# Both merge-gate products of a hybrid decoder layer in the seven-product scheme, with sums made on the fly

## The chip, the cores and the metric

The kernel runs on one core of one Trainium2 chip. The metric is the device time of one execution in microseconds (us). The kernel before takes 618.91 us, the median of three runs (618.71 to 619.36).

## The reference, cut to what matters

The layer takes 512 tokens of 1024 channels (float32). It normalises them to `h`, projects `h`, runs two branches (a gated linear recurrence giving `y_a` and a latent attention giving `y_b`, both 512 x 1024), and merges the branches by two sigmoid gates:

```python
h      = rms_norm(x, norm_g)
proj   = h @ w_in                       # its last 2 * 1024 columns are glog
gates  = sigmoid(glog + b_gate).reshape(B, S, 2, D_MODEL)
merged = gates[:, :, 0] * (y_a @ w_proj_a) + gates[:, :, 1] * (y_b @ w_proj_b)
x      = x + merged @ w_out
return rms_norm(x, final_norm_g)
```

The change is about the two products that make `glog`: 512 x 1024 times 1024 x 1024, once for each gate.

## The kernel before, in words

Every large product is made of three matmuls per block: each operand is split into a high part (rounded to the matmul's reduced float32 format) and a low part (the rest), and high x high, high x low and low x high are summed in PSUM. A split of a weight is one cast on ACT (`split` L155, `load_w` L113) and one subtraction on DVE (L156, L114). The normalised tokens lie split and transposed in `hT` (8 blocks of 128 channels by 512 tokens, high and low).

`proj_ch` (L122) is the ordinary product: for 256 output columns it loads two weight pieces of 512 KB, splits them, and issues 48 matmuls of 128 x 128 weights with 512 tokens streamed (lines 90 to 92). `gates` (L709) calls it four times for a gate and puts tanh on the result (ACT, L715). So one gate is 192 matmuls of 512 columns.

`ch_product` (L870) is one product of the seven-product (Strassen) scheme: the 1024 x 1024 weight is cut in four 512 x 512 blocks and the 512 tokens in two halves of 256; seven products of block sums replace eight. One product is 48 matmuls with 256 tokens streamed. In the kernel before two products use the scheme: `y_a @ w_proj_a` (L914 to 931) and, by tokens, `merged @ w_out` (L1078 to 1107). Their block sums are made by DMAs that add into SBUF (`add_by_dma`, L800, POOL's queue).

The order of the end of the kernel before:

- attention, head by head; for the last head (`h + 1 == H`, L760) PE's order is written by hand: gate 0's first 256 columns, with the transposes of the last head's softmax (`mla_transpose`, L696) in the middle, then `mla_out` (lines 90 to 92 with `pt` and `v`)
- the other three column groups of gate 0 (L849), during which `ya` is split and summed and the blocks of `w_proj_a` are loaded (L791) and summed by DMA
- `w_proj_a` by the seven products, PE by hand
- `merge` (L938): for each of four column groups, gate 1's `proj_ch`, then `w_proj_b`'s `proj_ch`; meanwhile the blocks of `w_out` are loaded into `ya`, `yb` and two further tiles and summed by DMA
- `w_out`'s seven products, the residual and the last norm.

Each engine runs its instructions in the order in which the scheduler queued them. Four buffers each hold high and low weight pieces (`whi`, `wlo`), three hold raw pieces (`wraw`), so two products' weights are held at a time. PSUM has three banks for products (`mm_ps`) and five for the rest (`ax_ps`). Tiles of a later stage (`Pool`, "left" and "right") lie on memory that earlier tiles leave; the first write waits for the last reader of what lay there.

Of the kernel before, what the change touches and what calls it, by code (L numbers as in the profile page):

```python
# [9 lines left out]
F32 = mybir.dt.float32  # L10
F32R = mybir.dt.float32r
# [7 lines left out]
P = 128  # L19
# [19 lines left out]
def hybrid_layer(ctx: ExitStack, tc: tile.TileContext, a):  # L39
# [698 lines left out]

    mw = Pool("mla", "right")
    ybp = Pool("ybp", "left")  # L740
    yb = ybp.tile([P, H, S], F32, "yb")
    qp, nope, pn = early
    late = None
    for h in range(H):
        pools = (ma_pool, mw)
        if h:
            pn = mla_scores(h, pools[h % 2], *nope, qp, h + 1 == H)
        if h + 1 < H:
            if h % 2:
                qp = mla_rope((h + 1) // 2)  # L750
        if h:
            z = mla_gate(h)
        if h:
            if h + 1 < H:
                nope = mla_nope(h + 1, pools[(h + 1) % 2])
            mla_out(*late)
            if h % 4 == 0:
                v = mla_values(h)
        hook = lambda: mla_transpose(pn)
        if h + 1 == H:  # L760
            with tc.manual_schedule(engines={mybir.EngineType.PE}):
# [63 lines left out]
    def a_tile(nm):  # L830
        return [yap.tile([P, 4, 256], F32R, f"{nm}{i}") for i in range(2)]
# [5 lines left out]
    def branch_blocks():  # L837

        return [yap.tile([P, 4, 512], F32, f"x{i}") for i in range(4)]

    x1, x2, x3, x4 = branch_blocks()
    p11, p12, p22, s1, s2 = [a_tile(n) for n in ("p11", "p12", "p22", "s1", "s2")]
    y11, y12, y21, y22 = blocks(ya)
    w_pa = a["w_proj_a"][0]
    with tc.issue_after(last_split[0].ins):
        for src, to in ((y11, p11), (y12, p12), (y22, p22)):
            a_parts(src, to)
    g = first_gates
    for c in range(1, 4):  # L849
        g = g + gates(0, c, to=ma)  # L850
        if c == 1:
            load_block(x3, w_pa, 0, 1)
            load_block(x1, w_pa, 0, 0)
            for q in kh:
                minus(y22[:, q], y22[:, q], y21[:, q])
                split(s1[0][:, q], s1[1][:, q], y22[:, q])
                minus(y21[:, q], y11[:, q], y21[:, q])
# [294 lines left out]
```

## Time and profile before

| | before |
|---|---|
| median of three runs | 618.91 us |
| profiled execution, its own time | 619.32 us |
| its span, first to last instruction | 617.6 us |
| PE (TensorE matmul) busy | 98% |
| DVE (VectorE) busy | 65% |
| ACT (ScalarE) busy | 42% |
| POOL (GpSimd) busy | 19% |
| mean granted TensorE clock | 0.997 |
| read from HBM, written | 60.25 MB, 2.10 MB |

Rows of the profile name a line of the kernel (L878), an engine, an operation, and out<-in by the program's tile names. PEld is PE's weight load, which overlaps the matmuls. SPq, ACTq and POOLq are the queues from which DMAs are issued. A matmul's own duration holds its way through the array; what a matmul costs in a stream is the distance from one to the next. Times "at 413.7" are microseconds from the start of the span. The profiled execution is 0.41 us above the median, and 1.7 us of its time lie outside its span.

### The profile page before, as it was taken

How to read it: one execution, taken by the hardware profiler on the slowest of the kernel's cores; microseconds unless marked ns; L12 is line 12 of the kernel's file. 1: busy time of each engine (PE TensorE's matmuls, PEld its weight loads, DVE VectorE, ACT ScalarE, POOL GpSimd, SP SyncE). 2: the span in 40 equal slices, each digit the busy share in tenths (PEclk: the TensorE clock that was granted, in tenths of full speed). 3: DMA queues.
4: the chain of work that ended last, by engine and by line, in shares of the span. 5: the costliest groups of instructions: out<-in, count | busy, mean ns of one | idle time of the engine just before them, and what ended most of it. 6: DMA issues, size and time to landing. Idle time of an engine off the chain costs nothing.

```text
span 617.6 us, 8947 instructions
## 1 busy us (share of the span) xinstructions
PE 607.3 (98%) x3400; PEld 518.2 (84%) x3400; DVE 400.5 (65%) x633; ACT 260.4 (42%) x483; POOL 117.9 (19%) x219
## 2 busy tenths in 40 slices
PE   8999999999999999999999999999999999999995
PEld 4998888888888888888888888888899888888884
DVE  7727855498874639967677757458267742447895
ACT  5645143323144232346545555354354532334352
POOL 3106201231230032321314132101110012000021
PEclk9999999999999999999999999999999999999998
DMA  8325243223205202432232243239952799600403
GB/s 275 117 67 171 68 140 100 68 69 103 69 12 160 80 24 59 116 86 74 72 99 74 55 117 88 70 84 325 239 148 51 270 359 276 193 1 0 171 0 136
DMA packets 62377, 72.35 MB, mean 117 GB/s; under 512 B 6104, under 2 KB 48510, under 8 KB 62336
## 3 DMA queue, kind: packets, MB, share of 16 engines
q1 hardware_dynamic: 58476, 61.37, 31.9%
q0 software_dynamic: 2160, 7.87, 6.4%
q10 hardware_dynamic: 1700, 2.56, 1.4%
q8 instruction: 26, 0.43, 0.3%
q14 instruction: 15, 0.12, 0.1%
HBM read 60.25 MB, written 2.10 MB: 101 GB/s over the span
## 4 chain that ended last, share of the span: by engine, by line
PE 96%; DVE 2%; ACT 1%; DMA 0%; issue 0%; POOL 0%; POOLq 0%; ACTq 0%; DVEq 0%
PE mm_ps L90 23%; PE mm_ps L91 23%; PE mm_ps L92 23%; PE ax_ps L878 6%; PE ax_ps L986 4%; PE ax_ps L675 2%; PE mm_ps L266 2%; PE ax_ps L696 1%; PE ax_ps L536 1%; PE ax_ps L92 1%; PE ax_ps L91 1%; PE ax_ps L90 1%; PE mm_ps L878 1%; PE mm_ps L986 1%; PE ax_ps L538 1%; PE ax_ps L498 1%
## 5 line engine op out<-in xcount | busy, mean ns | idle before, releaser
L114 DVE TENSOR_TENSOR w_lo<-w_raw,w_hi 128x1024 fp32r<-128x1024 f32 (+3 forms) x86 | 101.8, 1187 | 104.9 <-ACT w_hi L113 97.7
L113 ACT CAST w_hi<-w_raw 128x1024 fp32r<-128x1024 f32 (+3 forms) x86 | 85.0, 991 | 160.0 <-PE mm_ps L91 89.7
L90 PE MATMUL mm_ps<-hT,w_hi 128*128 128x512 f32 x384 | 151.2, 394 | 0.0
L91 PE MATMUL mm_ps<-hT,w_hi 128*128 128x512 f32 x384 | 150.0, 391 | 0.0
L92 PE MATMUL mm_ps<-hT,w_lo 128*128 128x512 f32 x384 | 149.6, 391 | 0.0
L92 PEld LDWEIGHTS mm_ps<-hT,w_lo 128*128 128x128 f32 x384 | 72.1, 188 | 14.8
L90 PEld LDWEIGHTS mm_ps<-hT,w_hi 128*128 128x128 f32 x384 | 72.2, 188 | 14.5 <-DVE qn L156 0.2
L91 PEld LDWEIGHTS mm_ps<-hT,w_hi 128*128 128x128 f32 x384 | 72.2, 188 | 14.2
L92 PE MATMUL mm_ps<-w_hi,hT 128*128 128x512 f32 (+1 forms) x96 | 36.6, 383 | 0.0
L91 PE MATMUL mm_ps<-w_lo,hT 128*128 128x512 f32 (+1 forms) x96 | 36.5, 382 | 0.0
L90 PE MATMUL mm_ps<-w_hi,hT 128*128 128x512 f32 (+1 forms) x96 | 36.4, 386 | 0.0
L683 POOL TENSOR_SCALAR p<-p,sm 128x128 f32<-128x128 f32 (+3 forms) x28 | 17.0, 608 | 71.1 <-DVE sm L680 60.6
L681 ACT ACTIVATE p<-ax_ps,sm 128x128 f32<-128x128 f32 (+3 forms) x32 | 16.9, 530 | 28.0 <-DVE sm L680 26.5
L455 DVE RECIPROCAL tf<-pr 128x512 f32<-128x512 f32 x8 | 26.8, 3351 | 0.2
L90 PE MATMUL mm_ps<-yb,w_hi 128*128 128x512 f32 x64 | 24.9, 389 | 0.0
L91 PE MATMUL mm_ps<-yb,w_hi 128*128 128x512 f32 x64 | 24.9, 389 | 0.0
L92 PE MATMUL mm_ps<-yb,w_lo 128*128 128x512 f32 x64 | 24.9, 389 | 0.0
L90 PE MATMUL mm_ps<-cT,w_hi 128*128 128x512 f32 x52 | 20.7, 398 | 0.0
L92 PEld LDWEIGHTS mm_ps<-w_hi,hT 128*128 128x128 f32 x96 | 18.0, 188 | 3.0
L90 PEld LDWEIGHTS mm_ps<-w_hi,hT 128*128 128x128 f32 x96 | 18.0, 188 | 3.0
L91 PEld LDWEIGHTS mm_ps<-w_lo,hT 128*128 128x128 f32 x96 | 18.0, 188 | 2.9
L92 PE MATMUL mm_ps<-cT,w_lo 128*128 128x512 f32 x52 | 20.3, 390 | 0.0
(284 smaller groups left out, 1147.1 us busy)
## 6 DMA issues: line engine op xcount, KB each, us to landing
w_raw<-w_in SPq DMA_DIRECT2D x58, 512.0 KB, 3.8
x<-w_proj_a SPq DMA_DIRECT2D x10, 512.0 KB, 6.5
x<-x POOLq DMA_DIRECT2D x8, 512.0 KB, 9.4
w_raw<-w_proj_b SPq DMA_DIRECT2D x8, 512.0 KB, 9.9
w_raw<-w_proj_a SPq DMA_DIRECT2D x4, 512.0 KB, 11.2
ya<-w_out SPq DMA_DIRECT2D x4, 512.0 KB, 7.7
t<-w_out SPq DMA_DIRECT2D x4, 512.0 KB
yb<-w_out SPq DMA_DIRECT2D x4, 512.0 KB, 10.9
```

The costliest lines, as they stand in the source:

```text
L90: nc.tensor.matmul(ps, lh[lsl], rh[rsl], start=start, stop=False)
L91: nc.tensor.matmul(ps, lh[lsl], rl[rsl], start=False, stop=False)
L92: nc.tensor.matmul(ps, ll[lsl], rh[rsl], start=False, stop=stop)
L113: nc.scalar.copy(hi[:, :o], raw[:, :o])
L114: (lo_eng or nc.vector).tensor_tensor(lo[:, :o], raw[:, :o], hi[:, :o].bitcast(F32), op=ALU.subtract)
L266: nc.tensor.matmul(ps, hT[l][:, 4 * kh + k, t * P : t * P + P], c_hl[kh][r][:, k * 256 : k * 256 + 256], start=kh == 0 and kind == 0 and k ...
L455: nc.vector.reciprocal(rp[:], pr[:])
L675: nc.tensor.matmul(sps[:, :n], qh[:, bl], kpe[x][:, :n], start=False, stop=x == 1)
L681: nc.scalar.activation(p[:, :n], sps[:, :n], AF.Exp, scale=SCALE, bias=sm[:, 1:2], accum_out=sm[:, 2:3])
L683: (nc.vector if final else nc.gpsimd).tensor_scalar(p[:, :n], p[:, :n], sm[:, 3:4], 0.5, op0=ALU.mult, op1=ALU.mult)
L878: nc.tensor.matmul(ps[:, o], w[k // 2][i][:, k % 2, cols], ap[j][:, k], start=not banks and c == 0 and n == 0, stop=n == 11, skip_group_ch ...
L986: nc.tensor.matmul(ps[:, o : o + n], ap[i][:, k, t * P : t * P + P], w[k // 2][j][:, k % 2, o : o + n], start=fresh and c == 0, stop=c == ...
```

## The change

`gates` goes; both gates are made with `strassen`, a function that holds the order of the seven products for gate 0, gate 1 and `w_proj_a` alike. `strassen` works on one set of four weight blocks `x4` (1 MB each, `x0` to `x3` for the blocks 00, 01, 10, 11). Their sums are made in place by POOL (`plus`: two adds of 128 x 1024 per block) and each block, once split, is loaded again with the block of the next matrix (`renew`): gate 0, then gate 1, then `w_proj_a`. The token sums of `h` (`s1` to `s4`) are made once, with `whole` (POOL: high + low) and DVE, and serve both gates.

For gate 0 the first two products (`w11` with `h11`, `w21` with `h12`) stand where gate 0's first column group stood, around the last head's transposes, and come from `load_w`. The third product, `t1` times `s1`, needs the sum `x0 + x1` and the token sum `s1 = h22 - h21`.

```diff
-    def gates(b, c, hook=None, to=None):
-
-        res = []
-        for i, ps in enumerate(proj_ch(w_in, COL_G + b * D + c * 256, hT, hook)):
...
+    def plus(out, x, y):
+        for q in kh:
+            nc.gpsimd.tensor_tensor(out[:, q], x[:, q], y[:, q], op=ALU.add)
+
+    def strassen(x, ops, out, first=None, between=(), mat=None, nxt=None):
...
+        y11, y12, y22, s1, s2, s3, s4 = ops
+        if first is None:
+            w11, w21 = w_parts(x00), w_parts(x10)
+            u = ch_product(w11, y11, copied("c11", 1.0))
+        else:
+            u = first
+        run(1)
+        plus(x00, x00, x01)
+        t1 = w_parts(x00)
+        if first is None:
+            ch_product(w21, y12, closed("c11", 0, 0, 1.0, out), tile=mm_tile)
+        run(2)
+        plus(x00, x00, x11)
+        plus(x01, x01, x11)
+        t2 = w_parts(x00)
+        r = ch_product(t1, s1, copied("c22", -1.0))
+        run(3)
+        if first is not None:
+            plus(x10, x10, x00)
+        w22 = w_parts(x11)
+        renew(1, 1)
+        ch_product(t2, s2, copied("c12", -1.0), u)
+        run(4)
+        if first is None:
+            plus(x10, x10, x00)
+        renew(0, 0)
+        t3 = w_parts(x01)
+        renew(0, 1)
+        ch_product(w22, s4, closed("c12", 4, 0, -1.0, out), r)
+        t4 = w_parts(x10)
+        renew(1, 0)
+        ch_product(t3, s3, closed("c22", 4, 1, -1.0, out), u)
+        ch_product(t4, y22, lambda b, ps: out(2 * b, 1, two(ps)), u)
...
         if h + 1 == H:
             with tc.manual_schedule(engines={mybir.EngineType.PE}):
-                pts = []
-                first_gates = gates(0, 0, lambda: pts.extend(hook()))
+                pts, later = [], []
+                w11, w21 = pieces(gate_w[0], 0, 0), pieces(gate_w[0], 1, 0)
+                u = ch_product(w11, h11, copied("c11", 1.0))
+                ch_product(w21, h12, lambda b, ps: later.append((b, ps)), tile=mm_tile, hook=lambda: pts.extend(hook()))
                 mla_out(h, pts, v, z)
...
+    for i, j in ((0, 0), (0, 1), (1, 1), (1, 0)):
+        load_block(x4[2 * i + j], gate_w[0], i, j)
...
+    def whole(out, hl):
+        nc.gpsimd.tensor_tensor(out, hl[0].bitcast(F32), hl[1].bitcast(F32), op=ALU.add)
+
+    e1, e2 = [g_rows[:, 2 * i : 2 * i + 2].rearrange("p a (b c) -> p (a b) c", c=256) for i in range(2)]
+    e3 = wraw.tile([P, WCH], F32, tag="raw", name="e3")[:].rearrange("p (k c) -> p k c", k=4)
+    whole(e1, h22)
+    nc.vector.tensor_tensor(e2, h21[0].bitcast(F32), h21[1].bitcast(F32), op=ALU.add)
+    whole(e3, h11)
+    minus(e1, e1, e2)
+    a_parts(e1, s1)
+    minus_minus(e1, e1, e3)
+    a_parts(e1, s2)
...
+    with tc.manual_schedule(engines={mybir.EngineType.PE}):
+        strassen(x4, h_ops, gate_out(0, lambda j: ma[:, j]), first=u, nxt=gate_w[1])
...
+    with tc.manual_schedule(engines={mybir.EngineType.PE}):
+        strassen(x4, h_ops, gate_out(1, lambda j: g1[j]), nxt=w_pa)
...
+    with tc.manual_schedule(engines={mybir.EngineType.PE}):
+        strassen(x4, (p1, p2, p3, p3, p4, p2, p1), gated,
+                 between={1: lambda: a_parts(y12, p1), 2: lambda: a_parts(y21, p2), 3: lambda: a_parts(y22, p3)}.items())
...
     for n, c in enumerate((0, 2, 1, 3)):
-        for i, (g, ps) in enumerate(merge(1, c, ybs, a["w_proj_b"][0])):
+        for i, ps in enumerate(proj_ch(a["w_proj_b"][0], c * 256, ybs)):
```

`w_proj_b` stays an ordinary product and `w_out` stays as it was, but between them and gate 1 the order changes: all of gate 1 now stands ahead of `w_proj_a`, and `w_proj_b`'s four column groups follow each other.

Where the instructions stand now, at the three places of which the prediction speaks. First PE, from the end of the last head's attention output (`mla_out` of head 7: `pt` times `v`), before. `w_hi` is a weight piece of gate 0, `hT` the tokens:

```order
L90 MATMUL mm_ps_4095<-pt02_4059,v0_3474 128x256
L91 MATMUL mm_ps_4095<-pt12_4062,v0_3474 128x256
L92 MATMUL mm_ps_4095<-pt02_4059,v1_3475 128x256
L90 MATMUL mm_ps_4095<-pt01_4058,v0_3474 128x128
L91 MATMUL mm_ps_4095<-pt11_4061,v0_3474 128x128
L92 MATMUL mm_ps_4095<-pt01_4058,v1_3475 128x128
L90 MATMUL mm_ps_4146<-hT0_123,w_hi_4155 128x512
L91 MATMUL mm_ps_4146<-hT1_124,w_hi_4155 128x512
```

And the same place after the change, where `s00` and `s01` are the high and low part of the token sum `s1` and `wo_hi`, `wo_lo` the parts of `x0 + x1`:

```order
L91 MATMUL mm_ps_4156<-pt12_4115,v0_3474 128x256
L92 MATMUL mm_ps_4156<-pt02_4112,v1_3475 128x256
L90 MATMUL mm_ps_4156<-pt01_4111,v0_3474 128x128
L91 MATMUL mm_ps_4156<-pt11_4114,v0_3474 128x128
L92 MATMUL mm_ps_4156<-pt01_4111,v1_3475 128x128
L781 MATMUL ax_ps_4263<-s00_4192,wo_hi_4243 128x256 x2
L781 MATMUL ax_ps_4263<-s00_4192,wo_hi_4247 128x256 x2
L781 MATMUL ax_ps_4263<-s01_4193,wo_hi_4243 128x256 x2
L781 MATMUL ax_ps_4263<-s01_4193,wo_hi_4247 128x256 x2
L781 MATMUL ax_ps_4263<-s00_4192,wo_lo_4244 128x256 x2
```

What followed `mla_out` needed only weights and `hT`; what follows it now needs the token sum.

Second, POOL after the change, from the first token sum on (`e3` is h11, `g_rows` holds h22; `x0` to `x3` are the weight blocks; x2 is two halves):

```order
L914 TENSOR_TENSOR e3_4208<-hT0_123,hT1_124 128x1024
L813 TENSOR_TENSOR x0_4177<-x0_4177,x1_4178 128x1024 x2
L813 TENSOR_TENSOR x1_4178<-x1_4178,x3_4180 128x1024 x2
L813 TENSOR_TENSOR x0_4177<-x0_4177,x3_4180 128x1024 x2
L914 TENSOR_TENSOR g_rows_4207<-hT0_123,hT1_124 128x1024
L813 TENSOR_TENSOR x2_4179<-x2_4179,x0_4177 128x1024 x2
L914 TENSOR_TENSOR e3_4208<-hT0_123,hT1_124 128x1024
```

The scheduler queued the h22 sum, from which `s1` is made, behind six adds of weight blocks. In the built program it also waits for the last matmul of `mla_out` of head 7, because `g_rows` lies on memory that the attention's tiles held until then. POOL had no work but DMA issues in this stretch before.

Third, DVE after the change, from head 7's output on:

```order
L706 TENSOR_TENSOR yb_2664<-mm_ps_4156,z_3985 128x512
L919 TENSOR_TENSOR g_rows_4207<-hT0_123,hT1_124 128x1024
L156 TENSOR_TENSOR wo_lo_4256<-x0_4177,wo_hi_4255 128x1024
L156 TENSOR_TENSOR wo_lo_4260<-x0_4177,wo_hi_4259 128x1024
L740 TENSOR_TENSOR g_rows_4207<-g_rows_4207 128x1024
L740 TENSOR_TENSOR g_rows_4207<-e3_4208,g_rows_4207 128x1024
L156 TENSOR_TENSOR s01_4193<-g_rows_4207,s00_4192 128x512 x2
```

The first L740 row is h22 - h21; ACT's casts to `s00` and then DVE's `s01` follow it, with another subtraction queued between them.

More of the change, by code (lines that the diff above doesn't have):

```diff
@@ L835, in a_parts, with ch_product @@
             split(to[0][:, q], to[1][:, q], src[:, q])
[L837 to L857, printed above, removed]
[L858 to L870 removed]
+    def ch_product(w, ap, done, banks=None, tile=ax_tile, hook=None):
         res = banks or [tile() for _ in range(2)]
         for b, ps in enumerate(res):
+            if hook and b:
+                hook()
             for c in range(2):
@@ new lines, in hybrid_layer @@
+    gate_w = [w_in[:, COL_G + b * D : COL_G + b * D + D] for b in range(2)]
+    w_pa = a["w_proj_a"][0]
+    h11, h12, h21, h22 = zip(*[blocks(t) for t in hT])
+    mw = Pool("mla", "right")
+    ybp = Pool("ybp", "left")
+    yb = ybp.tile([P, H, S], F32, "yb")
+    qp, nope, pn = early
+    late = None
+    for h in range(H):
+        pools = (ma_pool, mw)
+        if h:
+            pn = mla_scores(h, pools[h % 2], *nope, qp, h + 1 == H)
+        if h + 1 < H:
+            if h % 2:
+                qp = mla_rope((h + 1) // 2)
+        if h:
+            z = mla_gate(h)
+        if h:
+            if h + 1 < H:
+                nope = mla_nope(h + 1, pools[(h + 1) % 2])
+            mla_out(*late)
+            if h % 4 == 0:
+                v = mla_values(h)
+        hook = lambda: mla_transpose(pn)
+        if h + 1 == H:
+            with tc.manual_schedule(engines={mybir.EngineType.PE}):
[3 more added lines that the diff above has]
+                ch_product(w21, h12, lambda b, ps: later.append((b, ps)), tile=mm_tile, hook=lambda: pts.extend(hook()))
+                mla_out(h, pts, v, z)
+        elif h:
+            late = (h, hook(), v, z)
+        else:
+            with tc.manual_schedule(engines={mybir.EngineType.PE}):
+                nope = mla_nope(1, pools[1])
+                v = mla_values(0)
+                late = (0, hook(), v, z)
@@ new lines, in hybrid_layer @@
+    mw.close()
+    ma_pool.close()
+    cpool.close()
+    xp = Pool("blocks", "right")
+    x4 = [xp.tile([P, 4, 512], F32, f"x{i}") for i in range(4)]
+    for i, j in ((0, 0), (0, 1), (1, 1), (1, 0)):
+        load_block(x4[2 * i + j], gate_w[0], i, j)
+    hs = Pool("h_sums", "right")
+    s1, s2, s3, s4 = [[hs.tile([P, 4, 256], F32R, f"s{n}{i}") for i in range(2)] for n in range(4)]
+    mp = Pool("merged", "left")
+    ma = mp.tile([P, KD, S], F32, "ma")
+    gp = Pool("gates", "left")
+    g_rows = gp.tile([P, 5, S], F32, "g_rows")
@@ new lines, in hybrid_layer, with gate_out, out @@
+    a_parts(e1, s2)
+    minus(e2, e3, e2)
+    whole(e3, h12)
+    minus_minus(e3, e3, e1)
+    a_parts(e3, s4)
+    a_parts(e2, s3)
+    def gate_out(b, rows):
+        def out(j, tok, src):
+            for i in range(2):
+                n = 8 * b + j + i
+                nc.scalar.activation(rows(j + i)[:, half_t[tok]], src[:, i], AF.Tanh, scale=0.5, bias=hb_gate[:, n : n + 1])
+        return out
+    for n, (b, ps) in enumerate(later):
+        closed("c11", 0, 0, 1.0, gate_out(0, lambda j: ma[:, j]))(b, ps)
@@ L935, in hybrid_layer @@
+    for q in kh:
+        minus_minus(y12[:, q], y12[:, q], y11[:, q])
+    ybs = hT
+    with tc.manual_schedule(engines={mybir.EngineType.PE}):
+        strassen(x4, (p1, p2, p3, p3, p4, p2, p1), gated,
+                 between={1: lambda: a_parts(y12, p1), 2: lambda: a_parts(y21, p2), 3: lambda: a_parts(y22, p3)}.items())
+    for h in range(H):
+        split(ybs[0][:, h], ybs[1][:, h], yb[:, h])
+    hs.close()
+    xp.close()
     b11, b21, b12, b22 = ya[:, 0:4], ya[:, 4:8], yb[:, 0:4], yb[:, 4:8]
```

120 lines of the change are left out of this document (30 added, 90 removed).

## The prediction

> **What bounds the kernel now.** I read the page first: busy shares, then the chain that ended last.
>
> ```profile
> PE 607.3 (98%) x3400; PEld 518.2 (84%) x3400; DVE 400.5 (65%) x633; ACT 260.4 (42%) x483; POOL 117.9 (19%) x219
> ...
> PE 96%; DVE 2%; ACT 1%; DMA 0%; issue 0%; POOL 0%; POOLq 0%; ACTq 0%; DVEq 0%
> ```
>
> PE is busy for 98% of the span and makes 96% of the chain: each matmul waits for the one before it, and nothing else decides. A change that takes matmuls away gains their distance, as long as PE goes on finding its operands ready. So I need two things: what the matmuls cost, and whether PE must wait in the new order. The chain in order of time gives the cost (start, length, what):
>
> ```profile
> 440.60 0.23 PE mm_ps L91
> 440.82 0.23 PE mm_ps L92
> 441.28 0.23 PE mm_ps L91
> ...
> 444.45 5.75 PE ax_ps L878 x48
> 450.20 5.76 PE mm_ps L878 x48
> ...
> 571.84 5.44 PE ax_ps L986 x24
> ```
>
> From one L91 to the next lie three matmuls of 512 columns and 0.68 us, so one costs 0.227. A product of the seven (48 matmuls of 256 columns, L878) costs 5.755, or 0.120 each: a little more than half of 0.227. The last stage, w_out, begins at 571.84 and the span ends at 617.6.
>
> **The matmuls.** Removed: two gates of 192 matmuls, 384 x 0.227 = 87.1 us. Added: fourteen products, 14 x 5.755 = 80.6. The gain is 6.5 us (1.05%) and no more: seven eighths of the columns, less the worse price of narrow matmuls. PE may lose 6.5 us in waits before the change costs time.
>
> **The small wait ahead.** In the old order 24 gate matmuls stood between the first matmul of head 6's output and head 7's third score block. In the new order the scores follow at once, and the bank that the third takes is one that DVE still has to read. The rows are from the timeline (start, length).
>
> ```profile
> 393.56 0.50 PE L90 MATMUL mm_ps<-pt,v 128*128 128x512 f32 x1
> ...
> 394.85 1.01 DVE L156 TENSOR_TENSOR pt<-ax_ps,pt 128x512 fp32r<-128x512 f32 x2
> ...
> 395.83 0.68 DVE L156 TENSOR_TENSOR pt<-ax_ps,pt 128x512 fp32r<-128x512 f32 x1
> ...
> 414.18 0.27 PE L92 MATMUL mm_ps<-pt,v 128*128 128x128 f32 x1
> ...
> 414.52 4.04 SPq L791 DMA_DIRECT2D x<-w_proj_a  x8
> ```
>
> DVE frees that bank about 395.5, PE comes at 394.1: 1.3 us lost, taken as certain. From 393.9 to 444.45, where w_proj_a begins, PE did 192 gate matmuls (43.5) and 7.05 us of attention. After: that same 7.05, two products (11.5) and 1.3, so head 7's output ends at 413.7 instead of 414.45. The last row shows what memory reuse means here: the w_proj_a blocks were issued at 414.52, as soon as the last attention matmul had ended, since they lie where attention tiles lay. The token sum h22 now lies there too.
>
> **The seam at 413.7.** Next on PE is t1 times s1. s1 needs four steps in a row: POOL's h22 sum, DVE's subtraction, ACT's casts, DVE's low part. POOL's is the one with no row of its size, so its nearest rows stand first (group rows: busy, mean ns; source row: min/median/max):
>
> ```profile
> L619 POOL TENSOR_TENSOR qr<-qr,qs 128x512 f32<-128x512 f32 x4 | 6.0, 1507 | 0.2
> L617 POOL TENSOR_TENSOR qr<-qr,qtab 128x512 f32<-128x512 f32 x4 | 5.8, 1459 | 19.2 <-DMA qs<-qr 19.2
> L618 POOL TENSOR_TENSOR qs<-qs,qtab 128x512 f32<-128x512 f32 x4 | 5.8, 1451 | 0.0
> ...
> L619 POOL TENSOR_TENSOR qr<-qr,qs x4: 1280/1298/2151, 263.0 to 370.0; 128x512 f32<-128x512 f32 x4
> ...
> L472 POOL TENSOR_TENSOR k<-ko,gh x8: 612/706/1475, 69.9 to 247.5; 128x256 f32<-128x256 f32 x8
> ```
>
> The least time doubles with the size (612, then 1280), so 1024 columns cost at least 2.56 us; twice the mean of three rows, 1472, is 2.94; twice the worst, 4.3. I take 2.94, as DVE works beside it here as it did there. The Trainium skill (GPSIMD Engine Reference, 3.1 Elementwise) gives 4497 ns for a two-input add of 2048 columns: an estimate of 2.25 us for 1024, below twice the trace's least for 512; by it the sum below would be 2.2 us lower.
>
> The other steps have rows:
>
> ```profile
> L156 DVE TENSOR_TENSOR wo_lo<-x,wo_hi 128x1024 fp32r<-128x1024 f32 x10 | 12.0, 1220 | 8.7 <-ACT wo_hi L155 8.7
> ...
> L794 DVE TENSOR_TENSOR ya<-ya 128x512 f32<-128x512 f32 x4 | 2.7, 683 | 0.0
> ...
> L155 ACT CAST wo_hi<-x 128x1024 fp32r<-128x1024 f32 x10 | 10.0, 1046 | 10.2 <-PE ax_ps L878 8.0 <-PE mm_ps L878 2.2
> ...
> L155 ACT CAST s<-ya 128x512 fp32r<-128x512 f32 x6 | 3.7, 619 | 2.5 <-DVE ya L794 1.4 <-DVE ya L798 1.1
> ...
> w_raw<-w_in SPq DMA_DIRECT2D x58, 512.0 KB, 3.8
> x<-w_proj_a SPq DMA_DIRECT2D x10, 512.0 KB, 6.5
> ...
> 392.31 0.62 PE L696 MATMUL ax_ps<-ident,p 128*128 128x128 f32 x4
> ```
>
> (The DMA rows give the median us from issue to landing, the last row is from the timeline.)
>
> Ahead of the h22 sum POOL has six adds, queued in order. The blocks x0, x1 may load once head 6's transposes (392.31 to 392.9) have read the memory under them; at 0.5 us an issue (4.04 for eight) the third DMA, half of x1, goes out at 393.8 and lands 3.8 to 6.5 later: 399. Then:
>
> - 399.0 plus four adds: 410.8 (x3, issued from 398.4, is there by then)
> - the fifth and sixth add also wait for the split of the first sum, 409.8 and about 412.9 by DVE's queue; POOL is later: 416.6
> - h22: 419.6; DVE subtracts, 1.22: 420.8; ACT casts the first half, 0.62: 421.4, and PE starts.
>
> PE has then been idle for 7.7 us. It runs two matmuls, and gets the second half of s1's high part at 422.0 and its low part, behind another subtraction, at 422.7 and 423.35; its first twelve matmuls end at 424.1, 1.25 later than in a stream. If POOL needs only 2.56, the sixth add starts at 412.9 and h22 ends at 418.0, 1.6 earlier. Even with POOL at DVE's 1.22 the tail after 413.7 would be 1.22 + 1.22 + 0.62 + 1.25 = 4.3.
>
> **The clock after the wait.** The trace has no such wait, but its start and its end show what one does:
>
> ```profile
> 2.43 1.91 PE L231 MATMUL ax_ps<-zero 128*128 128x512 bf16 x4
> ...
> 11.84 1.04 PE L231 MATMUL ax_ps<-zero 128*128 128x512 bf16 x4
> ...
> 610.00:617.00 7.00, 0.07 (x1) 0.00 (x0) 1.80 (x4) 1.85 (x4) 1.57 (x4) 0.74 0.39 150
> ```
>
> The first four matmuls take 1.91 us, the same four at 11.84 take 1.04; after the last matmul the granted clock (third number from the end) falls to a mean of 0.74 over 7 us: half, for half of it. So after 7.7 us PE resumes slowly. The bounds are 0 (the clock holds) and 2 us (half speed for 4 us, as from 2.43 to 6.5); part of it lies in the 1.25 above. I take 1.2. The Trainium skill (TensorE: Matmul & The Clock Gate, Part 1) says that after an idle window of about 3.4 us the clock is halved until about 3.4 busy us have passed: an estimate of 1.7 us, and a sum 0.5 higher.
>
> **What stays hidden.** Later seams have slack, by the same prices. In each later set (40.3 us) POOL has eight adds (23.5). Its tightest: x0 of the next matrix is split 24.9 us after t1's start in the set before; six adds later, 42.5, and a cast and subtraction on, 44.8, t2's low part is ready, where PE wants it at 47.0 (its high part 43.6, wanted 46.2). That breaks above 3.3 us per add. Reloads of blocks have over 10 us against 6.5 to land. DVE's added splits find room (65% busy). In w_proj_b's 43.5 us six blocks of w_out must load and be summed by DMA, which took 44 us before (first issue 481.97; last add 516.1 plus 9.6); they now start 9 us ahead of the stage, so about 35 us into it; DVE's queue holds one add that waits for them ahead of the close of a bank that PE wants at 35. I take 0, at most 4.
>
> ```profile
> 481.97 2.26 SPq L791 DMA_DIRECT2D ya<-w_out  x4
> ...
> t<-t POOLq DMA_DIRECT2D x2, 512.0 KB, 9.6
> ...
> 516.11 1.76 POOL L802 DMA_DIRECT2D yb<-yb  x1
> ```
>
> **The sum.** -6.5 + 1.3 + 7.7 + 1.25 + 1.2 = +4.95 us: the profiled execution's 619.32 becomes 624.3, and against the median, 0.41 lower, 618.91 + 4.9 = 623.8.
>
> **Rivals.**
>
> 1. *No loss* (chance 0.10 within 0.2%, 0.05 faster). If the seam cost nothing, the change gives 6.5 - 1.3 = 5.2 us: 613.7. The mechanism: POOL's adds run at DVE's pace and the clock holds, so the seam is 4.3 and the sum -0.9: 618.0, which is "same"; faster needs a seam under 4.0, an add of at most 0.9 us, or a wait that isn't there. For it: POOL's spans are rough. Against it: 1280 ns is the least row of half the size.
> 2. *Quick POOL* (inside my own range): 2.56 an add and a held clock, -6.5 + 1.3 + 6.1 + 1.25 = +2.15: 621.0. It decides if DVE does not disturb POOL here.
> 3. *Slow POOL* (chance 0.15). At 3.6 us per add the seam grows by 7 x 0.66 = 4.6, and both later sets stall for about 1.3 at t2: +4.95 + 7.2 = +12, 631. For it: 2151 ns is the worst half size. It decides from 3.3 us on. A DMA too late for w_proj_b's end adds up to 4 here as well.
>
> **Chances and range.** Forecast (a seam of 9 to 13 us, 620.5 to 627): 0.70. A measurement of this kernel can tell about 0.2%, 1.2 us, from no change. Faster 0.05, same 0.10, slower 0.85. The range takes in rival 2 below and part of rival 3 above: 619.8 to 629.0; no change at all and the worst stalls are left out.
>
> **What would show it.** PE's row should fall below 607 us busy and its share of the span below 97%; a gap of 6 to 9 us in one place, ahead of the first L781 matmul on s, released by ACT's cast, behind DVE L740, behind POOL L914. L813 and L914 adds of 2.6 to 3.3 us. The granted clock below 1 right behind the gap. Elsewhere L781 should go at 5.755 per 48. I'm wrong if that gap is under 5 us, or if PE also stops in the second and third set.

## The result, and the profile after

The changed kernel takes 655.33 us (median of six runs, 653.68 to 656.19), against 618.88 us for the kernel before in the same session: a ratio of 1.058, interval 1.057 to 1.060. The profiled execution has a span of 653.8 us where before had 617.6. The forecast had +4.95 us, the chip shows +36.2.

The page of the changed kernel begins with the busy shares and, in its fourth part, the chain that ended last:

```profile
PE 612.0 (94%) x3688; PEld 534.4 (82%) x3688; DVE 467.9 (72%) x670; ACT 284.5 (44%) x531; POOL 188.8 (29%) x238
...
PE 83%; DVE 11%; issue 3%; ACT 2%; POOL 0%; POOLq 0%; ACTq 0%; DVEq 0%
```

PE is no longer the whole chain: DVE has 11% of it. POOL has almost nothing of it, although POOL got the new work. The waits of PE say where this is (us in total, times, longest):

```profile
PE ax_ps L781 <- ACT s L155: 13.8, 1, 13.8
PE ax_ps L781 <- DVE wo_lo L156: 12.0, 5, 5.2
PE ax_ps L781 <- ACT wo_hi L155: 3.4, 4, 1.4
PE ax_ps L90 <- DVE pt L156: 1.6, 1, 1.6
...
PE ax_ps L1027 <- DVE xr L1061: 0.8, 2, 0.6
```

These five lines are 31.6 us. The expected gap ahead of `t1` is there (first row), but of 13.8 us instead of 7.7. The second and third row were expected to be nothing; four of the five waits in the second lie inside the product of `t2`, in the second and in the third set. The fourth row is the small wait that was priced at 1.3.

The rest is in PE's busy time, most of it through the clock. The busy time should have come to 607.3 less 6.5, 600.8 us; it is 612.0, 11.2 us more. 31.6 + 11.2 - 6.5 is 36.3, the whole difference. The windows show the clock (us, then the busy time of PE, PEld, DVE, ACT and POOL; the third number from the end is the granted clock):

```profile
396.00:398.00 2.00, 2.00 (x8) 1.71 (x7) 1.99 (x10) 0.81 (x4) 0.00 (x0) 0.54 1.05 408
398.00:400.00 2.00, 2.00 (x9) 1.63 (x8) 0.29 (x2) 0.45 (x2) 0.93 (x1) 0.61 0.82 309
...
420.00:430.00 10.00, 0.97 (x4) 0.95 (x4) 9.96 (x5) 1.57 (x3) 7.19 (x3) 0.50 0.35 98
430.00:440.00 10.00, 10.00 (x70) 9.76 (x70) 9.32 (x11) 5.62 (x10) 2.41 (x1) 0.82 0.02 7
...
480.00:490.00 10.00, 5.82 (x33) 5.33 (x32) 9.88 (x10) 5.39 (x9) 1.80 (x1) 0.66 0.39 116
...
530.00:540.00 10.00, 2.55 (x12) 2.05 (x11) 10.00 (x11) 3.25 (x5) 3.55 (x2) 0.63 0.17 55
```

Narrower windows find four stretches at half the clock while PE still had matmuls to make, each around a wait or just behind one:

```profile
396.14:399.55 3.41, 3.41 (x10) 2.79 (x9) 1.93 (x9) 1.24 (x4) 0.48 (x1) 0.50 1.03 396
420.03:433.69 13.66, 4.66 (x19) 4.40 (x20) 13.01 (x9) 2.86 (x6) 7.69 (x4) 0.50 0.27 77
481.47:488.30 6.83, 3.82 (x16) 3.53 (x17) 6.71 (x8) 4.79 (x8) 0.33 (x1) 0.50 0.36 119
532.67:542.91 10.24, 5.08 (x22) 4.79 (x23) 9.38 (x12) 1.18 (x3) 0.88 (x1) 0.50 0.16 54
```

PE is busy for 17.0 us in them; at full clock that work takes half, so 8.5 of the 11.2 us are the clock. The other 2.7 are not accounted for one by one.

In every window of 10 us in which PE stands for more than 1 us, DVE is busy for 9.88 us or more, with few instructions: five in 10 us at 420, where before a DVE instruction of 1024 columns took 1.22 us. So DVE is what ends last, and its instructions are slow. The groups and the sources name them (group row: busy, mean ns; source rows: min/median/max):

```profile
L813 POOL TENSOR_TENSOR x<-x,x 128x1024 f32<-128x1024 f32 x24 | 70.2, 2952 | 61.0 <-DVE wo_lo L156 52.7
```

```profile
L156 DVE TENSOR_TENSOR wo_lo<-x,wo_hi x38: 1209/1218/3423, 410.1 to 553.6; 128x1024 fp32r<-128x1024 f32 x38
...
L156 DVE TENSOR_TENSOR hT<-yb,hT x8: 680/2554/2904, 471.1 to 520.3; 128x512 fp32r<-128x512 f32 x8
```

The mean POOL add is 2.952 us, and 2.94 had been taken. But the splits on DVE, 1.22 and 0.68 us by themselves, take up to 3.4 and 2.9. Two single-engine timelines around the gap show when (start, length). POOL:

```profile
417.30 3.33 POOL L914 TENSOR_TENSOR g_rows<-hT,hT 128x1024 f32<-128x1024 f32 x1
...
420.60 3.31 POOL L813 TENSOR_TENSOR x<-x,x 128x1024 f32<-128x1024 f32 x1
...
423.87 3.31 POOL L813 TENSOR_TENSOR x<-x,x 128x1024 f32<-128x1024 f32 x1
```

and DVE in the same stretch:

```profile
418.36 3.36 DVE L156 TENSOR_TENSOR wo_lo<-x,wo_hi 128x1024 fp32r<-128x1024 f32 x1
...
421.64 3.35 DVE L156 TENSOR_TENSOR wo_lo<-x,wo_hi 128x1024 fp32r<-128x1024 f32 x1
...
424.92 3.36 DVE L740 TENSOR_TENSOR g_rows<-g_rows 128x1024 f32<-128x1024 f32 x1
```

Read the ends. POOL's add ends at 420.63, DVE's split at 421.72, POOL's next at 423.91, DVE's at 424.99, POOL's at 427.18, DVE's subtraction at 428.28: one end of each in turn, POOL's 2.2 us after DVE's, DVE's 1.1 us after POOL's. That is about what each takes in a stream of its own: 1.14 from one such DVE instruction to the next where no add ran (427.78 to 428.92 in experiment 7), 2.34 from POOL's first add (399.07, 2.39 long) to its second. So they did not run side by side: each instruction's recorded time holds its wait for the other engine's whole instruction. The h22 sum of POOL was ready at 420.63, one microsecond later than forecast; the subtraction that it released ended 7.65 us later: two splits stood ahead of it, the first held by the h22 sum itself and the second by a block add, and then it was held by a block add too.

The Trainium skill states this ("SBUF — State Buffer", section "Who interferes with whom"): a DVE instruction with two inputs in SBUF and a GpSimd instruction that reads SBUF need a shared read port, which one holds for its whole instruction while the other is fully blocked. The alternation above agrees; the experiments test it.

In the later sets the chain in order of time (start, length) shows how this reaches PE:

```profile
471.16 5.62 DVE hT L156 x2
476.79 0.60 DVE c L803
477.39 1.94 DVE hT L156
...
479.51 2.84 DVE hT L156
482.35 0.60 DVE c L803
482.95 2.28 DVE wo_lo L156 x2
485.27 6.74 PE ax_ps L781 x43
```

`t2`'s low parts (482.95) stand in DVE's queue behind four splits of `yb` that only `w_proj_b`, some 80 us later, needs. Each of the four (2.88, 2.90, 2.27, 2.84) waited for a POOL add. The two closes of banks (L803), which have one input in PSUM, took 0.60 here; the first of them stood beside a running POOL add.

### The profile page after: what moved, and what is told of

Read it like the earlier page. It is cut to its first block, busy times and chain, and to the rows that moved or that the text cites. A ratio compares the mean times of both kernels' runs of the same rounds, so it can differ in the third digit from the quotient of the medians.

```text
span 653.8 us, 9649 instructions
## 1 busy us (share of the span) xinstructions
PE 612.0 (94%) x3688; PEld 534.4 (82%) x3688; DVE 467.9 (72%) x670; ACT 284.5 (44%) x531; POOL 188.8 (29%) x238
## 3 DMA queue, kind: packets, MB, share of 16 engines
q10 hardware_dynamic: 1700, 2.56, 1.4%
## 4 chain that ended last, share of the span: by engine, by line
PE 83%; DVE 11%; issue 3%; ACT 2%; POOL 0%; POOLq 0%; ACTq 0%; DVEq 0%
PE mm_ps L90 17%; PE mm_ps L91 17%; PE mm_ps L92 17%; PE ax_ps L781 13%; DVE wo_lo L156 3%; PE ax_ps L1027 2%; DVE hT L156 2%; PE ax_ps L675 2%; PE mm_ps L266 1%; PE ax_ps L696 1%; PE ax_ps L536 1%; DVE s L156 1%; PE ax_ps L90 1%; PE ax_ps L92 1%; PE ax_ps L91 1%
## 5 line engine op out<-in xcount | busy, mean ns | idle before, releaser
L90 PE MATMUL mm_ps<-hT,w_hi 128*128 128x512 f32 x320 | 126.2, 395 | 0.0
L91 PE MATMUL mm_ps<-hT,w_hi 128*128 128x512 f32 x320 | 125.2, 391 | 0.0
L92 PE MATMUL mm_ps<-hT,w_lo 128*128 128x512 f32 x320 | 124.6, 392 | 0.0
L813 POOL TENSOR_TENSOR x<-x,x 128x1024 f32<-128x1024 f32 x24 | 70.2, 2952 | 61.0 <-DVE wo_lo L156 52.7
L781 PE MATMUL ax_ps<-s,wo_hi 128*128 128x256 f32 x448 | 67.9, 296 | 17.2 <-ACT s L155 13.8
L781 PEld LDWEIGHTS ax_ps<-s,wo_hi 128*128 128x128 f32 x448 | 61.9, 203 | 18.5 <-ACT s L155 13.9
L92 PEld LDWEIGHTS mm_ps<-hT,w_lo 128*128 128x128 f32 x320 | 60.2, 188 | 12.3
L90 PEld LDWEIGHTS mm_ps<-hT,w_hi 128*128 128x128 f32 x320 | 60.2, 188 | 11.9
L91 PEld LDWEIGHTS mm_ps<-hT,w_hi 128*128 128x128 f32 x320 | 60.2, 188 | 11.7
L156 DVE TENSOR_TENSOR wo_lo<-x,wo_hi 128x1024 fp32r<-128x1024 f32 x38 | 58.1, 1561 | 14.3 <-ACT wo_hi L155 14.1
L155 ACT CAST wo_hi<-x 128x1024 fp32r<-128x1024 f32 x38 | 38.3, 1046 | 29.5 <-POOL x L813 10.4
L781 PE MATMUL ax_ps<-s,wo_lo 128*128 128x256 f32 x224 | 39.3, 298 | 12.0 <-DVE wo_lo L156 12.0
L781 PEld LDWEIGHTS ax_ps<-s,wo_lo 128*128 128x128 f32 x224 | 33.1, 204 | 13.2 <-DVE wo_lo L156 13.2
L90 PE MATMUL mm_ps<-w_hi,hT 128*128 128x512 f32 (+1 forms) x96 | 36.4, 386 | 0.0
```

The lines of the kernel that those rows point to most:

```text
L90: nc.tensor.matmul(ps, lh[lsl], rh[rsl], start=start, stop=False)
L91: nc.tensor.matmul(ps, lh[lsl], rl[rsl], start=False, stop=False)
L92: nc.tensor.matmul(ps, ll[lsl], rh[rsl], start=False, stop=stop)
L155: last_split[0] = nc.scalar.copy(hi, src)
L156: nc.vector.tensor_tensor(lo, src, hi.bitcast(F32), op=ALU.subtract)
L781: nc.tensor.matmul(ps[:, o], w[k // 2][i][:, k % 2, cols], ap[j][:, k], start=not banks and c == 0 and n == 0, stop=n == 11, skip_group_ch ...
```

## The experiments

My theory, called A in the texts on record: the two engines take turns, because POOL's adds read SBUF and DVE's operations have two inputs there, and DVE's in-order queue hands the delay on to operands that PE waits for. The rivals: POOL is merely slow or in the way of memory however it works; the delay comes from the length of DVE's queue or the place of the token sums in it; the adds could be made elsewhere and the gain of 6.5 us be had. Times are medians beside the kernel before on the same chip (619.0 to 619.3 us).

**1 (e1). The block sums left out** (the adds in `plus` are gone, everything else stays).

```diff
-            nc.gpsimd.tensor_tensor(out[:, q], x[:, q], y[:, q], op=ALU.add)
+            pass
```

> The twelve in-place sums of weight blocks are left out (the products then use the blocks as loaded), all else stays: loads, splits, token sums, PE's order. POOL keeps only the three token sums. Theory A (turn-taking: a DVE operation with two SBUF inputs and a POOL add of SBUF tiles cannot run at the same time, each waits for the other's end): with the adds gone the DVE subtractions are back at 1.22 and 0.69 us, no stall in the later sets, and only the seam ahead of t1 stays, by the h22 sum, one subtraction and one cast, 4 to 6 us plus about 2 us of restart: 613.7 + 7 = 620 to 622. Theory B (the adds are merely too slow and too many for POOL): also 620 to 622, so this run is the floor for both. Theory C (the block loads, the reload in place or the added splits are what is late): the stalls of 8.0 and 11.5 us in the two later sets stay, 638 or more.

Measured: 627.31 us, 1.0136 (1.0121 to 1.0151). 28 of the 36 us belong to the adds. The source rows of DVE are back at their own length, and PE no longer waits for a low part:

```profile
L156 DVE TENSOR_TENSOR wo_lo<-x,wo_hi x38: 1215/1221/1228, 405.4 to 524.9; 128x1024 fp32r<-128x1024 f32 x38
...
L156 DVE TENSOR_TENSOR hT<-yb,hT x8: 681/684/687, 460.3 to 499.1; 128x512 fp32r<-128x512 f32 x8
```

But the kernel is still slower than before: with block sums that cost nothing, the gap ahead of `t1` is 6.5 us, its product takes 2.7 more than 5.76, and the two later sets 1.46 and 0.72 more than seven products. The 0.72 are no loss: three matmuls of the next stage stand inside the last product of `w_proj_a`, as they did before, where that set also took 41.0 us. `w_out` took 47.5 instead of 45.9. This floor was above the 620 to 622 that I had expected, and it is where the gain of 6.5 goes even without POOL's block sums (POOL still makes the three token sums here).

**2 (e2). POOL writes, but reads nothing** (each add becomes three fills of the same tile, 2560 columns in all; the sums are left out).

```diff
-            nc.gpsimd.tensor_tensor(out[:, q], x[:, q], y[:, q], op=ALU.add)
+            for part_q in (out[:, q], out[:, q], out[:, q][:, 0:1]):
+                nc.gpsimd.memset(part_q, 0.01)
```

> Each POOL add of 128x1024 is replaced by three POOL fills of the same tile (128x1024 twice, 128x512 once, about 2.4 us together by the 0.53 us that a fill of 512 took in the kernel before): POOL is as busy, in the same place of its queue, with the same waits on the splits, but reads nothing from SBUF (the sums are left out). Theory A: DVE's subtractions beside it take 1.22 and 0.69 us again, POOL gets through its queue at 2.4 us, the later sets do not stall; the seam stays near my forecast since h22 is still behind the fills: 621 to 626. Theory B (POOL's slowness alone): the seam stays 12 us or more and the later sets stall at t2 again: 640 to 655, with DVE's subtractions beside POOL still at 2.3 to 3.4 us.

Measured: 627.65 us, 1.0139 (1.0123 to 1.0156), the floor of the first run, and like it above the range expected. POOL is as loaded as with the adds (176 us busy, against 189), at the same places of its queue. 41 of DVE's operations with two SBUF inputs overlapped a fill; one of them was long, and that one stood beside the h22 sum, which still reads. Being slow, or writing, isn't what POOL does to these operations: it must read.

```profile
L156 DVE TENSOR_TENSOR wo_lo<-x,wo_hi x38: 1215/1222/3361, 408.6 to 526.0; 128x1024 fp32r<-128x1024 f32 x38
```

For another kind of operation, writing was enough. A `tensor_scalar` of DVE with one SBUF input (0.42 in run 1) waited here beside a token sum and then through seven fills in a row, the last of which ended at 406.75:

```profile
399.77 7.20 DVE L683 TENSOR_SCALAR p<-p,sm 128x384 f32<-128x384 f32 x1
```

PE was not held up by it here.

**3 (e11). POOL reads one input** (each add becomes x times 1 plus 0; the sums are left out).

```diff
-            nc.gpsimd.tensor_tensor(out[:, q], x[:, q], y[:, q], op=ALU.add)
+            nc.gpsimd.tensor_scalar(out[:, q], x[:, q], 1.0, 0.0, op0=ALU.mult, op1=ALU.add)
```

> As the kernel after, but each POOL add of two tiles becomes a POOL operation with one SBUF input (times one plus zero, in place), so that the sums are left out while POOL still reads SBUF. The fills, which read nothing, cost 627.6. Theory A (what counts is that POOL reads SBUF): DVE's subtractions beside it still wait for a whole POOL operation, now a shorter one of some 1.3 us: single subtractions of 1.22 become up to 2.5, time 630 to 640. Theory A2 (only two inputs on both sides collide): DVE keeps 1.22 and 0.69, 626 to 629.

Measured: 627.64 us, 1.0138 (1.0119 to 1.0156). The turns are there, and short: POOL's operation takes 1.05 to 1.97 us, 1.17 in the median, and the splits of `yb`, 0.68 by themselves, are held to at most 1.53.

```profile
L156 DVE TENSOR_TENSOR wo_lo<-x,wo_hi x38: 1206/1218/2066, 407.0 to 526.6; 128x1024 fp32r<-128x1024 f32 x38
...
L156 DVE TENSOR_TENSOR hT<-yb,hT x8: 676/1104/1530, 462.0 to 502.4; 128x512 fp32r<-128x512 f32 x8
```

The time alone would speak for the rival, A2 (626 to 629; for A I had expected 630 to 640): what decides for A are these rows. PE is reached by none of it. So one read input is enough to block, and the price is the length of the POOL instruction that DVE meets; it costs time only where DVE's slack ends.

**4 (e9). The adds in the kernel before**, where nothing else is changed: twelve adds on a spare tile that nothing waits for, placed in `w_proj_a`'s stage.

```diff
+    spare = yap.tile([P, WCH], F32, "spare")
+    nc.gpsimd.memset(spare[:], 0.0)
...
-        add_by_dma(x1, x2)
+        for q in kh:
+            last_add = nc.gpsimd.dma_start(x1[:, q], x2[:, q], accum_op=ALU.add)
+        with tc.issue_after(last_add.ins):
+            for _ in range(12):
+                nc.gpsimd.tensor_tensor(spare[:], spare[:], spare[:], op=ALU.add)
```

> The disputed cost by itself, in the kernel before: twelve POOL adds of 128x1024 on a spare tile that nothing waits for, queued behind the last DMA sum of w_proj_a (issued at 458.5), so that they run beside w_proj_a's subtractions on DVE. Theory A: of DVE's operations with two SBUF inputs from 460 to 490 (subtractions of 1.22 and 0.68 us) several take 2 to 3.4 us; those with one input in PSUM (0.69) do not; the adds take 2.3 us alone and up to 3.5 beside DVE; time plus 0 to 4 us. Theory B (no turn-taking, POOL is just slow): DVE keeps 1.22 and 0.68 throughout, the adds take 2.3 to 2.9, time plus 0.

Measured: 632.28 us, 1.0207 (1.0189 to 1.0225): 13.0 us lost to results that nobody uses, all of it inside `w_proj_a` (54.2 us from its first matmul to the next stage, 41.0 before). I had expected less; the mechanism is A's, its reach is larger. DVE's splits of L156, at most 1.226 in the kernel before, now reach 2.9:

```profile
L156 DVE TENSOR_TENSOR wo_lo<-x,wo_hi x10: 1212/1768/2914, 450.1 to 488.2; 128x1024 fp32r<-128x1024 f32 x10
...
L156 DVE TENSOR_TENSOR s<-ya,s x6: 683/684/2379, 421.2 to 469.2; 128x512 fp32r<-128x512 f32 x6
```

The waits of PE in this run fall on closes of banks and token splits of DVE, which no POOL instruction feeds:

```profile
PE ax_ps L880 <- DVE c L908: 5.4, 1, 5.4
PE ax_ps L880 <- DVE s L156: 3.4, 2, 1.9
```

This is the cleanest proof: same program, no added dependence, only a second reader of SBUF.

**5 (e3). The adds on DVE itself.**

```diff
-            nc.gpsimd.tensor_tensor(out[:, q], x[:, q], y[:, q], op=ALU.add)
+            nc.vector.tensor_tensor(out[:, q], x[:, q], y[:, q], op=ALU.add)
```

> The block sums move from POOL to DVE: 24 adds of 128x1024 at 1.22 us, 29.3 us more for DVE, none for POOL. Theory A: the pair of an add and a subtraction, which took 3.3 us in turns, takes 2.44, and nothing waits for a whole add of 2.3 us; the later stalls of 8.0 and 11.5 us fall under 2 us each, the seam to 6 to 8 us: 620 to 627. Theory D (DVE is then the bound: its queue is full in this stretch whoever adds): stalls remain in every set, 632 to 645.

Measured: 637.02 us, 1.0293 (1.0278 to 1.0308). DVE gets 24 instructions more, and the kernel is 18 us faster than with POOL making them. An add takes 1.22, the splits 1.21 to 1.24, and PE's waits for `wo_lo` fall from 12.0 to 3.2; the gap is 9.2. What is left is DVE's in-order queue, on which the adds stand ahead of what PE needs; the time lies where it was expected for a DVE that is full whoever adds (632 to 645), and not where A alone had it.

**6 (e4). The adds by DMA** (accumulating into SBUF, as the kernel before did).

```diff
-            nc.gpsimd.tensor_tensor(out[:, q], x[:, q], y[:, q], op=ALU.add)
+            nc.gpsimd.dma_start(out[:, q], (y if x is out else x)[:, q], accum_op=ALU.add)
```

> The block sums are made by DMAs that add into SBUF, as the kernel before made those of w_proj_a: no engine works on them. Theory A: DVE is undisturbed, a sum of a block takes 9.6 us from issue to landing instead of 6 us in turns; two sums and two splits per set fit into 40 us: later stalls below 2 us, the seam 6 to 9 us: 620 to 626. Theory E (a sum by DMA waits behind the block loads): t1 or t2 late in each set by more than 4 us, 630 to 645.

Measured: 634.15 us, 1.0243 (1.0228 to 1.0259). The later sets are near the floor (+2.15 and +0.72), the first isn't. Its gap of 5.6 us is not of the DMA's making (6.5 without block sums), but `t1`'s product takes 5.4 us more and the rest of the set 4.5. PE waits there for 4.3 us in all, for low parts of token sums that stand on DVE behind splits of blocks, and the half clock follows; the casts of `t2`'s block had waited 4.0 us for its sum, which lands 5.8 us after its issue (median of all 24). The time is in the range of the rival, a DMA sum that comes too late (630 to 645).

**7 (e5). The token sum `s1` made early, adds on POOL.** `h22 - h21` is made by three DVE operations ahead of the gap, in a free weight buffer (the other token sums go to DVE too):

```diff
+    e3 = wraw.tile([P, WCH], F32, tag="raw", name="e3")[:].rearrange("p (k c) -> p k c", k=4)
+    whole(e3, h22)
+    minus(e3, e3, h21[0].bitcast(F32))
+    minus(e3, e3, h21[1].bitcast(F32))
     mw.close()
...
-    whole(e1, h22)
...
-    minus(e1, e1, e2)
-    a_parts(e1, s1)
+    a_parts(e3, s1)
```

> Only the first token sum changes: s1 = h22 - h21 is made by three DVE operations in a buffer that is free before head 7's output (h22's parts added, then h21's two parts subtracted), so that only its casts still wait for the last attention matmul; the other token sums go to DVE too. The block sums stay on POOL. Theory A (turn-taking): the seam shrinks from 13.8 us but not away, since t1's own subtractions and casts still share DVE and POOL with the adds; the stalls of 8.0 and 11.5 us at t2 in the later sets stay: 640 to 648. Theory F (the seam is the whole story, the later stalls are echoes of it): 622 to 630.

Measured: 654.1 us, 1.0576 (1.0554 to 1.0599): nothing won, against 7 to 15 us expected. `t1` starts at 418.53 instead of 429.03, and then stands 7.7 us in its middle, for the low part of `s1`. That part is behind two token sums in DVE's queue, each in turns with a POOL add:

```profile
418.81 2.41 DVE L864 TENSOR_TENSOR g_rows<-hT,hT 128x1024 f32<-128x1024 f32 x1
...
421.14 3.37 DVE L864 TENSOR_TENSOR g_rows<-hT,hT 128x1024 f32<-128x1024 f32 x1
...
424.43 2.82 DVE L156 TENSOR_TENSOR s<-e,s 128x512 fp32r<-128x512 f32 x1
```

The gap moved by one operand. The order isn't the cause as long as the adds are there.

**8 (e6). Both: DMA adds and the early `s1`** (the edits of 6 and 7 together).

> The early s1 and the block sums by DMA together, everything else in the order that the scheduler gives. Theory A: no POOL add is left, so the later sets run as in the run with sums by DMA alone; the first set still loses some us, since ACT's casts of t1 stand behind the cast of s1 and the tanh, and t2's sum starts only after t1's split: 624 to 630. If the seam of 5.6 us was due to the token sum alone: 620 to 623.

Measured: 630.4 us, 1.0174 (1.0161 to 1.0188). Now the early `s1` is worth 3.8 us; `t1` starts at 418.89, but its product takes 12.3: its weight's casts stand on ACT behind those of `s1` and four gate activations, PE waits 2.2 us inside the product for their parts, and most of its matmuls run at half the clock. The time is just above the 624 to 630 expected.

**9 and 10 (e8, e10). A version meant to beat both.** DMA adds; `s1` and `s2` early; the last head's output moved into a first product, so that no gap is left at its end; `t2` made in its own block; ACT and DVE ordered by hand in the first set.

```diff
-                ch_product(w21, h12, lambda b, ps: later.append((b, ps)), tile=mm_tile, hook=lambda: pts.extend(hook()))
-                mla_out(h, pts, v, z)
+                pts.extend(hook())
+                ch_product(w21, h12, lambda b, ps: later.append((b, ps)), tile=mm_tile, hook=lambda: mla_out(h, pts, v, z))
...
+    with tc.manual_schedule(engines={mybir.EngineType.PE, mybir.EngineType.DVE, mybir.EngineType.Activation}):
+        strassen_first(x4, (h22, s1, s2, s3, s4), gate_out(0, lambda j: ma[:, j]), u, gate_w[0], gate_w[1],
+                       (token_sums, sum_4, sum_3))
```

> The version that the runs point to: no adds on POOL (block sums by DMA), for gate 0 the sum of t2 in a block of its own so that it doesn't wait for t1's split (one block more is loaded), s1 and s2 made before head 7's output ends, that output moved ahead of the second half of the second product, and DVE's and ACT's order in gate 0 written by hand. If theory A and the account of the seam hold, what is left is the gain of 5.2 us less some 3 us (bank and cast waits of gate 1's last products and the last stage, as in the run without sums) and up to 2 us at the seam: 615.5 to 619. If an unseen cost of the seven products themselves is left, 622 or more.

Measured: 628.18 us, 1.0141 (1.0116 to 1.0167). The gap is gone (`t1` starts at 415.03 and takes 6.6), but 6.0 us come back in the rest of the first set, where casts stand behind token sums in my order, and 5.05 in the second, whose first block I load last. The next kernel mends these: `w21` ahead of `w11`, the blocks of gate 1 loaded in the order in which they are wanted, closes and sums in another order.

```diff
-                w11, w21 = pieces(gate_w[0], 0, 0), pieces(gate_w[0], 1, 0)
-                u = ch_product(w11, h11, copied("c11", 1.0))
+                w21, w11 = pieces(gate_w[0], 1, 0), pieces(gate_w[0], 0, 0)
+                ch_product(w21, h12, copied("c11", 1.0), tile=mm_tile)
...
+        load_block(xb, nxt, 0, 0)
```

> The version with sums by DMA again, with the places at which its first run still waited put right: the second product now goes first, on the banks of the plain products (so that head 7's third score block has matmuls ahead of it and no stall of 1.6 us comes at 393.6), ACT's and DVE's order in gate 0 lets no cast wait behind a token sum, and gate 1's first block is loaded into the slot that comes free first. If the remaining time was in these orders: 616.5 to 619.5, gate 0's products at 5.8 to 6.2 us each; if something else holds the products up (DMA queues full, ACT and DVE too busy), 622 to 628 as before.

Measured: 627.25 us, 1.0134 (1.0115 to 1.0152). The later sets are at the floor; the first wait is gone, but the transposes of the last head wait 3.2 us for its softmax, into which the early token sums have moved on DVE, the first set still gives away 3.9 from `t1` on, and `w_out` is 2.5 longer. Both were misses: most of what was taken out of one seam came up at the next.

**11 and 12 (e12). Gate 1 alone.** Gate 0 is an ordinary product as before, so that no seam lies at the attention's end and the token sums are made well ahead, on DVE; gate 1 and `w_proj_a` go by the changed kernel's `strassen`. Once with the adds on POOL:

> The same with the block sums on POOL, as in the change. Theory A: both sets that are left stall at t2 as they did there, by 8.0 and 11.5 us (perhaps less in the first, whose blocks are loaded early): 632 to 641. If the stalls came from gate 0's delays (the seam) and not from POOL and DVE taking turns: 618 to 622.

and once by DMA, with the edit of 6:

> One half of the change alone: gate 0 as an ordinary product again (so that the token sums are made behind 32 us of other matmuls and there is no seam), gate 1 and w_proj_a by the seven products on one set of blocks, block sums by DMA, token sums on DVE. Theory A with the account of the seam: the gain is half, 43.5 - 40.3 = 3.2 us, less 1.4 us in gate 1's last two products and 1.5 to 2 us in the last stage, which the runs without POOL adds lost too: 617.5 to 620. If the seven products on the tokens of h cost time by themselves: 622 or more.

Measured: 638.05 us, 1.0301 (1.0287 to 1.0316) with POOL, 619.34 us, 1.0006 (0.9994 to 1.0017) by DMA. 18.7 us hang on one line of code, without any gap at the seam. With POOL, the waits of PE and the splits of DVE are those of the changed kernel:

```profile
L156 DVE TENSOR_TENSOR wo_lo<-x,wo_hi x28: 1207/1217/3436, 428.7 to 536.6; 128x1024 fp32r<-128x1024 f32 x28
...
L156 DVE TENSOR_TENSOR hT<-yb,hT x8: 678/2576/2910, 452.5 to 502.7; 128x512 fp32r<-128x512 f32 x8
```

```profile
PE ax_ps L791 <- DVE wo_lo L156: 11.6, 5, 5.2
PE ax_ps L791 <- ACT wo_hi L155: 2.0, 3, 1.1
```

By DMA, no split of L156 is over 1.226 and PE's waits on products are 0.9 in all. The one gate's gain of 3.3 us is eaten by gate 1's 1.44 and by `w_out`, 48.1 instead of 45.9: a tie. No version of mine beats the kernel before.

## Why the prediction was wrong, step by step

| step | forecast, us | measured, us |
|---|---|---|
| matmuls | -6.5 | -6.5 |
| wait ahead of head 7's third score block | +1.3 | +1.6, and 1.5 by the clock behind it |
| gap ahead of `t1` | +7.7 | +13.8 |
| lag in `t1`'s product and clock | +1.25 + 1.2 | +2.4 |
| second set (gate 1) | 0 | +9.45 |
| third set (`w_proj_a`, 53.2 against 41.0 before) | 0 | +12.2 |
| `w_proj_b`, `w_out`, end | 0, at most 4 | +1.9, all in `w_out` |
| sum | +4.95 | +36.4 (the spans differ by 36.2) |

- **The matmuls.** Right: undisturbed products start 5.76 us apart, as 5.755 was priced.
- **The small wait.** Right in place and nearly in size (1.6). Not foreseen: the clock stood at half for 3.4 us behind it (396.14 to 399.55). In five other kernels with the same wait (1, 2, 5, 6 and 7) it did not, so these 1.5 us do not follow from the wait alone.
- **The gap: right in its place and its chain, and in POOL's part by luck.** The POOL adds were in the forecast order, and h22, the seventh, was done at 420.63 (forecast 419.6). But the first four adds took 2.45 each instead of 2.94, and the fifth and sixth then waited 2.58 and 1.16 for DVE's splits, where the forecast had POOL as the later one: two errors that nearly cancelled. The step that failed comes behind it: "DVE subtracts, 1.22: 420.8". DVE was done at 428.28. The price of the POOL add (2.94) came out on the mean (2.952) for a wrong reason: alone, an add takes 2.36 to 2.41, below the 2.56 that was taken as the least and near the estimate of 2.25 that I had worked out from the Trainium skill (GPSIMD Engine Reference, 3.1 Elementwise) and set aside; the rest of the mean is waiting for DVE. And as DVE waits for POOL in the same way, its price had to change as well. The failing sentence is "I take 2.94, as DVE works beside it here as it did there": it reads a disturbance of POOL by DVE into the rows and leaves out its other half.
- **What stays hidden: wrong.** "Later seams have slack, by the same prices": the prices were those of each engine alone. In the later sets DVE's queue holds splits of 0.68 and 1.22 ahead of `t2`'s low part; four of them grew to 2.3 to 2.9 in the second set. The two sets make some 22 of the 36 us, and with them came what the prediction had named as its refutation, a PE that also stops in the second and third set. The sentence "DVE's added splits find room (65% busy)" fails with it: DVE was busy for 9.88 to 10.00 us of each window of 10 in which PE stood for more than 1 us.
- **The clock.** In the gap's term right in sum (2.4 against 2.45, lag included), but by luck: 4.66 us of `t1`'s matmuls ran at half the clock, which makes 2.3 where 1.2 were priced, and the lag of the operands, priced at 1.25, was about 0.1. And the long later waits have slow stretches of their own; in sum the clock took 8.5 us.
- **The rivals.** The first and second are out. The third, slow POOL, named the two later stalls at `t2`, and its 3.3 us as the point from which they come; adds beside DVE took 2.8 to 3.3 (once 4.5). It was closest, but by the wrong cause, and gave 1.3 for stalls of about 9 and 12.

Could the profile before have shown it? There is a row, which I had not read. Its timeline at 328 has one POOL operation with two inputs beside one split of DVE:

```profile
327.87 1.30 POOL L619 TENSOR_TENSOR qr<-qr,qs 128x512 f32<-128x512 f32 x1
...
328.48 1.77 DVE L114 TENSOR_TENSOR w_lo<-w_raw,w_hi 128x1024 fp32r<-128x1024 f32 x1 [0.73 <-ACT w_hi L113]
```

POOL's ends at 329.17, DVE's at 330.25: 1.08 later, the same distance as in the changed kernel, and 1.77 instead of 1.22 for the split. The source row that I did quote (L619: 1280/1298/2151) carries the other half, a POOL operation that waited. A maximum so far above its median asks for the instruction beside it.

What the experiments show: that the adds on POOL cost 28 us (1), that they do it by reading SBUF (2, 3), that DVE's two-input operations are held without any dependence between the two (4), and that the same adds made elsewhere hold no split and cost 10 us (5, on DVE) or 7 (6, by DMA) over the floor instead of 28, and by DMA with gate 1 alone nothing that can be measured (12). That the blocked resource is a shared port is the Trainium skill's account ("SBUF — State Buffer", "Who interferes with whom"); the runs show turns of whole instructions, and no port. What stays open is the floor's last part: `w_out` is 1.9 us longer (47.8 against 45.9), which was seen, and not separated.

## What to carry to other kernels

An idle engine is no free engine: before work goes to POOL, look at what DVE does in that stretch, and if it has operations with two SBUF inputs (or a `tensor_scalar`, by the rows of the next section), price both engines as one queue, the sum of their durations, and not as two. Where such a pair exists in the trace, compare the longest row of a group with its median, and look at what the other engine did at that moment. And what a scheme saves in matmuls (6.5 us here) is only there if the sums that it needs are made off PE's path: with the block sums at no cost at all this one still lost 8.

## What the runs showed of the hardware that was not expected

- **The length of an instruction can be mostly waiting.** DVE splits of 0.68 us stand in the profile with 2.9, as busy time. DVE's busy share rose from 65% to 72%, by 67 us, of which about 33 (467.9 against 434.8 with the adds left out) are waiting for POOL.
- **Which operations are held.** Two SBUF inputs beside a POOL operation that reads: yes (all of the above). One of the inputs in PSUM: no (L803 took 0.68 at 476.71, between two held splits). Two SBUF inputs beside POOL fills: no (of 41 only the one that also met the h22 sum). A DVE `tensor_scalar` with one SBUF input, too, took 1.51 beside an add:

```profile
402.70 1.51 DVE L683 TENSOR_SCALAR p<-p,sm 128x512 f32<-128x512 f32 x1
```

  It takes 0.48 with POOL at rest (run 1, at 401.14). The Trainium skill ("SBUF — State Buffer", "Who interferes with whom") lists `tensor_scalar` among the operations that can enter a two-port mode and then contend; this row agrees. Beside fills it was held as well, for 7.20 us in run 2, and there without turns: it ended 0.22 us behind the last of seven fills in a row.
- **A short wait can halve the clock, or not.** The same wait of 1.6 us at 393.7 was followed by 3.4 us at half the clock in the profiled executions of the changed kernel and of runs 3, 8 and 9, and by full speed in those of runs 1, 2, 5, 6 and 7. The Trainium skill ("TensorE: Matmul & The Clock Gate", Part 1) puts the fall behind an idle window of about 3.4 us; here 1.6 were enough in four of nine.
